# 88 sums moved from VectorE to GpSimd in a hybrid decoder layer

## The chip, the cores and the metric

One Trainium2 chip, of which the kernel uses one core. The metric is the device time of one execution in microseconds. TensorE (PE) multiplies matrices into PSUM; VectorE (DVE), ScalarE (ACT) and GpSimd (POOL) work on the on-chip memories; SyncE (SP) only starts transfers. GpSimd starts transfers too, in the order of its own instruction queue.

## The reference

One layer over 2048 tokens of width 1024, in float32. After an RMS norm, one projection `w_in` gives nine groups of columns; two branches are computed, each with its own gate, and merged:

```python
h = rms_norm(x, norm_g)
u = einsum('bsd,dc->bsc', h, w_in)
v_c, b_c, c_c, z_c, q, k, v, z_a, gate_logits = split(u)

y_c = b_c * causal_depthwise_conv(c_c * v_c, conv_w) * silu(z_c)     # 3 taps
y_a = y_c @ w_conv_out

q, k = rms_norm per head (16 query heads, 4 key heads, 64 wide)
o = sliding_window_attention(q, k, v, sinks) * silu(z_a)             # window 128, a sink per head
y_b = o @ w_attn_out

g_a, g_b = split(sigmoid(gate_logits + gate_b))
out = x + (g_a * y_a + g_b * y_b) @ w_out
```

## The kernel before

**Tiles and units.** The tokens are worked on in two tiles of 1024. Within a tile the work is a list of units, written out by hand in `SEQ0` and `SEQ1`: each unit multiplies the tile's activations by 256 columns of a weight. Tile two's list begins `ga0+ga1 k q0 v q1 q2 cv0 q3` (a pair with + is interleaved), so keys, values and the four query units stand at its beginning. The last units (`o`) multiply by `w_out`.

**Seven products instead of eight.** A unit's 1024 x 256 weights are four blocks, by two halves of the depth and two halves of the columns; the activations are four chunks in the same way. Instead of eight block products, the kernel does seven, by Strassen's scheme in Winograd's form: some products take a block, others a sum or difference of blocks. A product is 12 matmuls (4 chunks of depth, and 3 terms, since each float32 operand is cut into a rounded high part and a low remainder). `sunit` writes the products in the order 1, 5, 6, 2, 7, 3, 4 into the PSUM banks X, V and Y.

So each unit needs *weight sums*: four instructions on 128 x 512 elements, in place in the two raw tiles `ra` and `rb` of the unit's weights, made in `pieces_of`, `sums`. Each step needs the one before it. The first three make the two blocks of products 5 and 6 (pair `s`), the fourth ends those of 7 and 3 (pair `t`). Afterwards ScalarE rounds a pair (`w.._sh`, `w.._th`, L362) and VectorE takes the remainder (`w.._sl`, `w.._tl`). The V product (5) uses pair `s`.

The right-hand operands need *chunk sums* in the same way: `sums_of` makes them for a set of activations, four per pair of chunks, in two steps `first` and `second`, and stores each in the DRAM array `sd`, from which `load_set` reads them when the set becomes operands. The sets are `("c", t)`, the conv branch's output of tile t; `("a", t)`, the attention branch's; `("h", 1)`, the normed tokens of tile two (made in `h_prep` during tile one); and `("w", 0)`, `w_out` (made in `w_prep`). Their argument `eng` is the engine that issues the stores: SyncE for `"c"`, GpSimd for the others.

**What sets the order.** The program is a list of *ticks*, one a product. In `run`, each tick emits a product with its evacuation (`fin`), then the rounding of the next piece of weights on ScalarE, up to three functions planned for that tick, the piece's VectorE half (`lo`; a piece of kind `sums` has only this), further planned functions, loads on SyncE, and finally up to four *woven* steps: chains of small instructions, such as those of a reciprocal square root, which also advance by one with each VectorE instruction that goes through `vec`. Weight pieces run ahead of their products as far as eight ring buffers allow. Every engine takes its instructions in this order.

In the units of tile two that matter here, `fin_q` evacuates a quarter of a query unit, splits it (`q_h` on ScalarE, `q_l` on VectorE) and writes it to DRAM by four transfers on GpSimd's queue (`q2d`, L855); `fin_k` writes `rkd` (L921), reads it back as `k_r` (L932) and writes `kd` (L776); `fin_v` has TensorE transpose the values (`ptv`, L708) from `v_t` and writes `vd` (L957). Attention for tile two starts at unit q3; its flips and returns (`fd`, `x`, L1073 and L1080), its masks (`affine_select`, L1101) and its sums of halves (`od`, L1134) are GpSimd's too.

Lines of helpers: L480 is every matmul of a unit, L262 every VectorE instruction through `vec`, L297 the rounding of `split`.

Of the kernel before, what the change touches and what calls it, by code (L numbers as in the profile page):

```python
# [105 lines left out]
def block_kernel(  # L106
# [12 lines left out]
    nc = tc.nc  # L119
# [18 lines left out]
    def slot(shape, dt, name):  # L138
        return big.tile(shape, dt, tag="big", name=name)
# [160 lines left out]
    def add(o, a, b, eng=None):  # L300
        return (eng or vec).tensor_tensor(out=o, in0=a, in1=b, op=ALU.add)

    def sub(o, a, b, eng=None):
        return (eng or vec).tensor_tensor(out=o, in0=a, in1=b, op=ALU.subtract)
# [45 lines left out]
    def wpair(name):  # L350
        return [wpool.tile([P, KP * UC], F32R, tag="w", name=f"{name}{i}") for i in "hl"]

    def pieces_of(n):

        kind, srcs, key = plan[n]
        name = "w" + "_".join(str(i) for i in key)
        w = {}

        def two(hi, lo, src):
            return (lambda: nc.scalar.copy(hi, src),  # L362
                    lambda: vec.tensor_tensor(
                        out=lo, in0=src, in1=hi.bitcast(F32), op=ALU.subtract))

        if kind == "R":
            return w, []

        if kind:
            def pair(h, m1, m2, nm):  # L370
                hi, lo = (v.rearrange("p (i j c) -> p i j c", i=2, c=P) for v in wpair(f"{name}_{nm}"))
                for i, m in enumerate((m1, m2)):
                    w[m] = (hi[:, i], lo[:, i])
                return two(hi, lo, raws[2 * n + h])

            if kind == "P":
                return w, [(2, 1, lambda h=h: pair(h, (h, 0), (h, 1), f"p{h}")) for h in range(2)]

            def single():
                if n in paired:  # L380
                    hl = [slot([P, KP, P], F32R, f"{name}_d{i}") for i in "hl"]
                else:
                    d = wpool.tile([P, 2, KP, P], F32R, tag="w", name=f"{name}_d")
                    hl = [d[:, 0], d[:, 1]]
                w[4] = tuple(hl)
                return two(*hl, raws[2 * n + 1][:, 1])

            def sums():
                ra, rb = raws[2 * n], raws[2 * n + 1]

                def f():
                    sub(ra[:, 0], ra[:, 0], rb[:, 0])
                    summed.append(vec.chain(
                        lambda: add(rb[:, 0], rb[:, 0], rb[:, 1]),
                        lambda: sub(rb[:, 1], rb[:, 1], ra[:, 0]),
                        lambda: sub(ra[:, 1], ra[:, 1], rb[:, 1])))

                return (lambda: None, f)

            summed = []  # L400

            def of_sums(*args):
                summed[0]()
                return pair(*args)

            def single_sums():
                hi, lo = single()
                _, f = sums()

                def g():  # L410
                    lo()
                    f()

                return hi, g

            first = [(1, 0, single), (0, 0, sums)] if n not in paired else [(0, 0, single_sums)]
            return w, [(2, 0, lambda: pair(0, 1, 2, "a")), *first,
                       (2, 1, lambda: of_sums(1, 5, 6, "s")), (2, 1, lambda: of_sums(0, 7, 3, "t"))]
# [259 lines left out]
    def put(n, f):  # L678
        at.setdefault(max(n, tick[0] + 1), []).append(f)
# [525 lines left out]

    def sums_of(key, j, r, eng, n0=None):

        def first():
            sub(r[0, 0], r[0, 1], r[0, 0])
            eng.dma_start(sd[key][0, j], r[0, 0])  # L1210
            sub(r[0, 1], r[1, 1], r[0, 1])
            eng.dma_start(sd[key][2, j], r[0, 1])

        def second():
            sub(r[1, 1], r[1, 1], r[0, 0])
            eng.dma_start(sd[key][1, j], r[1, 1])
            sub(r[1, 0], r[1, 0], r[1, 1])
            eng.dma_start(sd[key][3, j], r[1, 0])

        if n0 is not None:  # L1220
            put(n0, first)
            put(n0 + 1, second)
        return second, first
# [43 lines left out]
    def fin_z(t, j, src, nm, key, to, at_of, eng):  # L1267
        got, left = {}, [4]
        second, first = sums_of(key, j, got, eng)
        steps = [lambda: put(tick[0] + 1 + SUM_WAIT, second), lambda: put(tick[0] + 1, first)]  # L1270

# [79 lines left out]
    def w_prep(n0):  # L1351

        for j in range(KP):
            r = {}

            def ld(j=j, r=r):
                for p in range(2):
                    for q in range(2):
                        r[p, q] = slot([P, H], F32, f"wo_{j}_{p}_{q}")
                        c = 2 * j + p  # L1360
                        nc.gpsimd.dma_start(r[p, q], w_o[c * P : (c + 1) * P, hs(q)])

            put(n0 + W_AT[j], ld)
            sums_of(("w", 0), j, r, nc.gpsimd, n0 + W_AT[j] + 4)
# [30 lines left out]
    def h_prep(t, n0):  # L1395
# [11 lines left out]
        for j in range(KP):  # L1407
            r = {}

            def ld(q, j=j, r=r):  # L1410
                if j < H_UP and q == 0:
                    for p in range(2):
                        two = upool.tile([P, 2 * H + 2], F32, tag="u", name=f"h{t}_{2 * j + p}")
                        for k in range(2):
                            r[p, k] = two[:, hs(k)]
                for p in range(2):
                    if j >= H_UP:
                        r[p, q] = slot([P, H], F32, f"h{t}_{q}_{2 * j + p}")
                    c = 2 * j + p
                    nc.gpsimd.dma_start(  # L1420
                        r[p, q], xt2[c * P : (c + 1) * P, t * T + q * H : t * T + (q + 1) * H])

            def norm(q, j=j, r=r):
                for p in range(2):
                    x_norm(r[p, q], 2 * j + p, rb[q])
                    if (p, q) != (0, 1):
                        nc.gpsimd.dma_start(hd[t][2 * j + p, :, hs(q)], r[p, q])

            n = n0 + 1 + H_AT[j]
            for q in range(2):  # L1430
                put(n + q, lambda q=q, f=ld: f(q))
                put(n + q + 3, lambda q=q, f=norm: f(q))
            sums_of(("h", t), j, r, nc.gpsimd, n + 7)
# [8 lines left out]
    for t in range(NT):  # L1442
# [9 lines left out]
        for word in (SEQ0, SEQ1)[t].split():  # L1452
            both_ = word.split("+")
            for name in both_:
                if len(both_) > 1:
                    paired.add(len(plan))
                key, j = name.rstrip("0123456789"), int(name[-1]) if name[-1].isdigit() else None
# [144 lines left out]
    kv = KV()  # L1602
# [161 lines left out]
```

## Time and profile before

| | |
|---|---|
| median of 3 runs | 1891.34 us (1890.53 to 1893.8) |
| the profiled execution's own time | 1890.92 us |
| its span, first to last instruction | 1889.2 us |
| TensorE, matmuls | 1880.8 us busy, granted clock 1.000 |
| TensorE, weight loads | 1565.5 us busy |
| VectorE | 1540.0 us busy, 2536 instructions |
| ScalarE | 989.0 us busy |
| GpSimd | 728.7 us busy, 1038 instructions |
| DMA | 435.81 MB, 231 GB/s on average |

Busy times are shares of one profiled execution, and engines overlap. GpSimd's busy time counts the issue of its transfers (0.5 to 1.1 us each), which is most of its 1038 instructions. The ends of TensorE's matmuls are modelled, so its busy share alone does not say how fast it goes. Tile one's units take the first half of the span; tile two's begin at about 878 us, its key, value and query units near 916 us, and `w_out` begins at 1733 us.

### The profile page before, as it was taken

The numbers are of one execution on the slowest core, as the hardware profiler recorded it, in microseconds if no ns is written. First come the engines' busy times: TensorE is split into PE (matmuls) and PEld (weight loads), VectorE is DVE, ScalarE is ACT, GpSimd is POOL, SyncE is SP. The second block draws the span as 40 slices with busy tenths as digits, with TensorE's granted clock in tenths as the row PEclk, the third lists the DMA queues.
The fourth block names the chain that finished last, engine by engine and source line by source line (L and its number), as shares of the span: only waits on it lengthen the run. The fifth ranks groups of instructions, "written<-read, shape, count | busy, mean of one in ns | idle before, by whom it ended". The sixth has DMA issues, their size and how long they took to land.

```text
span 1889.2 us, 27869 instructions
## 1 busy us (share of the span) xinstructions
PE 1880.8 (100%) x8638; PEld 1565.5 (83%) x8638; DVE 1540.0 (82%) x2536; ACT 989.0 (52%) x1993; POOL 728.7 (39%) x1038
## 2 busy tenths in 40 slices
PE   9999999999999999999999999999999999999999
PEld 7888888888888888888887888888888888888887
DVE  7989888789878889887579988888877789887654
ACT  7665554567665345435455645556566436344321
POOL 1472454456667111021075445656666311121000
PEclk9999999999999999999999999999999999999999
DMA  8475566689888978889367557768888869899653
GB/s 307 123 217 170 144 175 190 182 246 302 251 246 258 318 267 301 286 286 296 112 184 221 182 170 207 206 164 238 243 241 255 269 245 347 318 281 272 223 173 110
DMA packets 261189, 435.81 MB, mean 231 GB/s; under 512 B 33649, under 2 KB 124785, under 8 KB 261041
## 3 DMA queue, kind: packets, MB, share of 16 engines
q1 hardware_dynamic: 202848, 314.13, 50.3%
q0 software_dynamic: 58048, 119.87, 24.0%
q8 instruction: 69, 1.13, 0.3%
q14 instruction: 80, 0.65, 0.1%
q10 hardware_dynamic: 144, 0.03, 0.0%
HBM read 279.48 MB, written 154.42 MB: 230 GB/s over the span
## 4 chain that ended last, share of the span: by engine, by line
PE 82%; issue 7%; DVE 5%; DMA 3%; POOL 2%; ACT 1%; SPq 0%; POOLq 0%; DVEq 0%; ACTq 0%
PE Y L480 30%; PE Vcv L480 5%; PE Xcv L480 5%; PE po L1118 2%; PE Xgb L480 2%; PE Xb L480 2%; PE Vgb L480 2%; PE Xz L480 2%; PE Vb L480 2%; PE Vz L480 2%; PE Vo L480 2%; PE Xo L480 2%; PE Xza L480 2%; PE Vza L480 2%; PE Vga L480 2%
## 5 line engine op out<-in xcount | busy, mean ns | idle before, releaser
L1080 POOL DMA_DIRECT2D x<-fd x256 | 144.1, 614 | 69.7 <-DMA fd<-f 24.9
L1101 POOL TENSOR_SCALAR_AFFINE_SELECT xh<-xh 64x512 fp32r<-64x512 f32 x64 | 66.7, 1043 | 133.1 <-DVE xl L262 96.2
L1053 ACT ACTIVATE p<-s,st,rq 128x128 f32<-128x128 f32 x256 | 113.0, 451 | 5.7 <-DMA fd<-f 3.7
L1073 POOL DMA_DIRECT2D fd<-f x64 | 39.0, 610 | 176.6 <-DVE f L262 152.3
L480 PE MATMUL Xcv<-oph,wcv_ah 128*128 128x512 f32 x256 | 79.5, 392 | 0.0
L1134 POOL DMA_DIRECT2D od<-o x64 | 69.4, 1092 | 24.6 <-DMA od<-o 20.4
L855 POOL DMA_DIRECT2D q2d<-q_h x64 | 44.3, 692 | 84.3 <-ACT q_h L850 81.9
L1324 POOL DMA_DIRECT2D md<-thyb x32 | 27.4, 872 | 103.3 <-DVE thyb L262 87.7
L1101 POOL TENSOR_SCALAR_AFFINE_SELECT xl<-xl 64x512 fp32r<-64x512 f32 x64 | 64.3, 1004 | 4.4
L1101 POOL TENSOR_SCALAR_AFFINE_SELECT yp<-yp 64x512 fp32r<-64x512 f32 x64 | 55.7, 870 | 5.0 <-ACT yp L1088 0.9
L1101 POOL TENSOR_SCALAR_AFFINE_SELECT yp<-xl 64x512 fp32r<-64x512 f32 x64 | 56.1, 876 | 3.1
L480 PEld LDWEIGHTS Xcv<-oph,wcv_ah 128*128 128x128 f32 x256 | 47.3, 188 | 9.4
L262 DVE SCALAR_TENSOR_TENSOR y<-u,cols,y 128x512 f32<-128x512 f32 x64 | 51.5, 804 | 3.7 <-ACT y L1163 2.5
L262 DVE TENSOR_TENSOR p<-p,st 128x512 f32<-128x512 f32 x64 | 49.7, 776 | 2.6
L262 DVE TENSOR_TENSOR opa<-ina,opa 128x512 fp32r<-128x512 f32 x56 | 36.2, 686 | 18.3 <-ACT opa L297 18.3
L1053 ACT ACTIVATION_READ_ACCUMULATOR p<-s,st,rq 128x1 f32 x256 | 50.9, 199 | 0.0
L362 ACT CAST wcv_sh<-wcv_raw 128x1024 fp32r<-128x1024 f32 x16 | 16.8, 1053 | 63.5 <-DVE wcv_raw L262 63.5
L480 PE MATMUL Xcv<-oph,wcv_al 128*128 128x512 f32 x128 | 49.8, 389 | 0.0
L855 POOL DMA_DIRECT2D q2d<-q_l x64 | 44.1, 689 | 12.6 <-DVE q_l L262 9.9
L1028 PEld LDWEIGHTS s<-kq,q 128*128 128x128 f32 x256 | 45.9, 189 | 2.2
L262 DVE STREAM_TRANSPOSE f<-p 128x512 f32<-128x512 f32 x64 | 45.4, 710 | 2.7 <-DVE p L262 0.2
L262 DVE TENSOR_TENSOR opc<-inc,opc 128x512 fp32r<-128x512 f32 x56 | 36.1, 686 | 13.9 <-ACT opc L297 13.8
(774 smaller groups left out, 6611.5 us busy)
## 6 DMA issues: line engine op xcount, KB each, us to landing
wcv_raw<-in_w_in SPq DMA_DIRECT2D x32, 512.0 KB, 4.2
q<-q2d SPq DMA_DIRECT2D x64, 256.0 KB, 4.7
v<-vd SPq DMA_DIRECT2D x128, 128.0 KB, 4.7
fd<-f POOLq DMA_DIRECT2D x64, 256.0 KB, 3.8
x<-fd POOLq DMA_DIRECT2D x256, 64.0 KB, 3.6
gd<-th SPq DMA_DIRECT2D x64, 256.0 KB, 3.4
wq_raw<-in_w_in SPq DMA_DIRECT2D x16, 512.0 KB, 5.0
q2d<-q_h POOLq DMA_DIRECT2D x64, 128.0 KB, 3.7
```

Of the source, the lines that this page charges most:

```text
L262: r = f(*args, **kw)
L362: return (lambda: nc.scalar.copy(hi, src), lambda: vec.tensor_tensor(out=lo, in0=src, in1=hi.bitcast(F32), op=ALU.subtract))
L480: nc.tensor.matmul(ps, lhsT=w[:, j, :], rhs=b[:, m, :], start=start and j == 0 and i == 0, stop=j == KP - 1 and i == 2, skip_group_check=n ...
L855: nc.gpsimd.dma_start(q2d[t][j][half, q * 2 * HB : (q + 1) * 2 * HB, i, e, :], src[HALVES[e]].bitcast(F32).rearrange("p (b x) -> p b x", x ...
L1028: nc.tensor.matmul(sp[:, h, c, skip : 3 * HD], lhsT=q2[:, h, c, :], rhs=kq[:, 0, keys], start=False, stop=c == 1)
L1053: nc.scalar.activation(out=p[:, i, :], in_=sg[:, i, HD : 3 * HD], func=AF.Exp, bias=st[:, 1, i : i + 1], scale=rv[:, i // 2, i % 2 : i % 2 ...
L1073: nc.gpsimd.dma_start(fd, f)
L1080: nc.gpsimd.dma_start(x[QUADS[k]], src[k])
L1101: nc.gpsimd.affine_select(out=d4, in_=s4, pattern=[[0, 2], [-32 * sg, 2], [0, G], [-sg, 32]], compare_op=ALU.is_gt if prev else ALU.is_ge, ...
L1118: nc.tensor.matmul(po[:, cs], lhsT=v2[:, kind, :], rhs=xx[:, :, h * HD : (h + 1) * HD], start=h == 0 and n == 0, stop=n == 2, skip_group_c ...
L1134: put(tick[0] + ADD_WAIT, lambda: nc.gpsimd.dma_start(to, o[UH].rearrange("p c e q -> p (c e) q"), accum_op=ALU.add))
L1324: nc.gpsimd.dma_start(md[t][k, :, hs(q)], m, accum_op=ALU.add)
```

## The change

In `sums`, the four weight sums of tile two's key, value and query units (six units; `key[1]` is the tile) are given to GpSimd, all four in the tick of the piece, and nothing is left for the woven chain. The condition's `key[0] in "kv"` holds for `k` and `v` alone. In `sums_of`, the sums are given to GpSimd wherever GpSimd issues the stores: sets `("a", 0)`, `("a", 1)`, `("h", 1)` and `("w", 0)`, 16 sums each. `sub` and `add` with an engine given bypass `vec`, so no woven step advances with them. The arithmetic is the same.

```diff
@@ in pieces_of, sums
                 def f():
+                    if (key[0] == "q" or key[0] in "kv") and key[1] == 1:
+                        eng = nc.gpsimd
+                        sub(ra[:, 0], ra[:, 0], rb[:, 0], eng)
+                        add(rb[:, 0], rb[:, 0], rb[:, 1], eng)
+                        sub(rb[:, 1], rb[:, 1], ra[:, 0], eng)
+                        sub(ra[:, 1], ra[:, 1], rb[:, 1], eng)
+                        summed.append(lambda: None)
+                        return
                     sub(ra[:, 0], ra[:, 0], rb[:, 0])
                     summed.append(vec.chain(
                         lambda: add(rb[:, 0], rb[:, 0], rb[:, 1]),
@@ def sums_of(key, j, r, eng, n0=None)
+        on = nc.gpsimd if eng is nc.gpsimd else None
+
         def first():
-            sub(r[0, 0], r[0, 1], r[0, 0])
+            sub(r[0, 0], r[0, 1], r[0, 0], on)
             eng.dma_start(sd[key][0, j], r[0, 0])
-            sub(r[0, 1], r[1, 1], r[0, 1])
+            sub(r[0, 1], r[1, 1], r[0, 1], on)
             eng.dma_start(sd[key][2, j], r[0, 1])
 
         def second():
-            sub(r[1, 1], r[1, 1], r[0, 0])
+            sub(r[1, 1], r[1, 1], r[0, 0], on)
             eng.dma_start(sd[key][1, j], r[1, 1])
-            sub(r[1, 0], r[1, 0], r[1, 1])
+            sub(r[1, 0], r[1, 0], r[1, 1], on)
             eng.dma_start(sd[key][3, j], r[1, 0])
```

## The prediction

> **What bounds the kernel now.** I read the page's head first, then two rows of the table of stretches (the stretch, its length, busy time and instructions of TensorE, its weight load, VectorE, ScalarE and GpSimd, the granted clock, the DMA share and rate), then TensorE's waits (total, times, longest), then the chain of waits, of which one row stands here for the pace.
>
> ```profile
> span 1889.2 us, 27869 instructions
> PE 1880.8 (100%) x8638; PEld 1565.5 (83%) x8638; DVE 1540.0 (82%) x2536; ACT 989.0 (52%) x1993; POOL 728.7 (39%) x1038
> ```
>
> ```profile
> 600.00:650.00 50.00, 50.00 (x225) 41.39 (x224) 43.78 (x60) 19.55 (x31) 18.22 (x26) 1.00 0.92 303
> 950.00:1010.00 60.00, 58.62 (x264) 47.34 (x263) 48.91 (x90) 34.02 (x58) 47.00 (x77) 1.00 0.78 227
> ```
>
> ```profile
> PE Y L1498 <- DVE zero L181: 1.5, 1, 1.5
> PE Vq L480 <- DVE wq_sl L262: 0.7, 1, 0.7
> PE Y L480 <- DVE yap L262: 0.7, 1, 0.7
> PE Vv L480 <- DVE wv_sl L262: 0.4, 1, 0.4
> PE Vq L480 <- ACT wq_sh L362: 0.3, 1, 0.3
> ```
>
> ```profile
> 1749.51 5.44 PE Xo L480 x24
> ```
>
> TensorE runs wall to wall at a granted clock of 1.00. Busy time alone would not prove it, because the ends of matmuls are modelled; the pace does: 24 matmuls in a row in 5.44 us, 0.227 us each, and a product of twelve (one tick of the kernel's clock) 2.72 us. The five waits shown are together 3.6 us, 1.5 of them the kernel's start. So VectorE, 82% busy, is not the bound, and freeing it can return little more than the rest, 2.1 us or 0.11%. A loss has no such ceiling: whatever makes TensorE wait is added to the end. Three of the five are for exactly what the change moves: weights made from sums of tile two's values and queries (wv_sl, wq_sl, wq_sh). They lie in 950 to 1010, where TensorE lost 1.38 us and where GpSimd is busiest: 47 of 60 us. All figures are made against this execution, 1890.92 us, its span of 1889.2 and 1.72 around it; the median of the runs is 1891.34, 0.42 above.
>
> **Price of one moved sum.** On VectorE a 128x512 sum takes 0.69 us. GpSimd has done no two-input arithmetic in this kernel; its nearest rows are the selects of the attention.
>
> ```profile
> L262 DVE TENSOR_TENSOR wk_raw<-wk_raw,wk_raw x3: 678/692/693, 903.9 to 906.1; 128x512 f32<-128x512 f32 x3
> L262 DVE TENSOR_TENSOR wq_raw<-wq_raw,wq_raw x21: 668/691/694, 63.8 to 1033.6; 128x512 f32<-128x512 f32 x21
> L1101 POOL TENSOR_SCALAR_AFFINE_SELECT xh<-xh x64: 742/764/1692, 188.9 to 1475.4; 64x512 fp32r<-64x512 f32 x64
> L262 DVE TENSOR_TENSOR p<-p,st x64: 691/692/1240, 166.2 to 1453.7; 128x512 f32<-128x512 f32 x64
> ```
>
> The columns are shortest, median and longest duration in ns, and the first and last start. A select passes 512 elements of one operand in 0.76 us. Lower bound p = 0.75: the second operand is free. Upper bound 1.5: it costs a second pass; beyond that 1.7, the longest select, which was held up by something. I take p = 1.15, the middle of 0.75 and 1.5. [...]
>
> **Weight sums, 24 instructions (six units of four).** Removed from VectorE: 24 x 0.69 = 16.6 us, which TensorE does not feel. Added on GpSimd: 24 x 1.15 = 27.6 us, in order behind its DMA issues. Three sums must end before ScalarE rounds the first pair of sums (wq_sh, wv_sh) and VectorE takes the remainder (wq_sl, wv_sl), which the V product needs. So I look for the place of each unit's sums in GpSimd's queue. For keys (VectorE's sums at 903.9 to 906.1) and query 0, the next unit, the queue is empty: the first row below says GpSimd had been idle for 62.83 us at 947.61. For query 3 (VectorE sums to 1033.6) it is empty too, 21.76 us idle before 1044.58. There the sums start as soon as their operands are free, and cost nothing; without that cover it would be the lateness found next, 2.4 to 4.2 us a unit. For values, query 1 and query 2 the queue is full:
>
> ```profile
> 947.61 0.75 POOL L855 DMA_DIRECT2D q2d<-q_h  x1 [62.83 <-ACT q_h L850]
> ...
> 953.58 0.70 POOL L855 DMA_DIRECT2D q2d<-q_l  x1
> 954.27 3.88 POOL L921 DMA_DIRECT2D rkd<-k_rt  x8
> ...
> 964.65 0.53 POOL L932 DMA_DIRECT2D k_r<-rkd  x1 [0.48 <-DMA q2d<-q_l]
> 965.50 0.52 POOL L932 DMA_DIRECT2D k_r<-rkd  x1 [0.33 <-DMA q2d<-q_h]
> 966.40 2.69 POOL L932 DMA_DIRECT2D k_r<-rkd  x5 [0.39 <-DMA q2d<-q_l]
> 969.98 2.50 POOL L957 DMA_DIRECT2D vd<-v  x4 [0.89 <-DVE v L262]
> ...
> 996.75 0.69 POOL L855 DMA_DIRECT2D q2d<-q_l  x1 [0.24 <-issue]
> 997.43 0.61 POOL L776 DMA_DIRECT2D kd<-k_h  x1
> ...
> 1044.58 0.58 POOL L1073 DMA_DIRECT2D fd<-f  x1 [21.76 <-DVE f L262]
> ```
>
> ```profile
> 955.30 1.05 ACT L362 CAST wv_sh<-wv_raw 128x1024 fp32r<-128x1024 f32 x1 [2.55 <-DVE wv_raw L262]
> ...
> 973.24 1.05 ACT L362 CAST wq_sh<-wq_raw 128x1024 fp32r<-128x1024 f32 x1 [1.03 <-DVE wq_raw L262]
> ...
> 976.41 0.59 ACT L582 COPY v_t<-Y 128x512 f32<-128x512 f32 x1
> ...
> 996.68 1.05 ACT L362 CAST wq_sh<-wq_raw 128x1024 fp32r<-128x1024 f32 x1 [1.56 <-DVE wq_raw L262]
> ```
>
> ```profile
> 957.66 0.50 PE L480 MATMUL Vv<-oph,wv_sl 128*128 128x512 f32 x1 [0.41 <-DVE wv_sl L262]
> ...
> 977.83 0.60 PE L708 MATMUL ptv<-ident,v_t 128*128 128x128 f32 x4
> ...
> 999.23 0.50 PE L480 MATMUL Vq<-oph,wq_sl 128*128 128x512 f32 x1 [0.71 <-DVE wq_sl L262]
> ```
>
> ScalarE's rounding has no slack: each of the three already sat waiting for VectorE's sums, and everything behind it on ScalarE waits too.
>
> *Values.* In the program the sums follow the eight q2d issues of query 0's first two quarters, so they take the place of the rkd issues at 954.27. Three of them end at 954.28 + 3p = 957.73; ScalarE had them at 955.30. TensorE was already waiting for the result (0.41 at 957.66): late by 3p - 1.02 = **2.43 us**.
>
> *Query 1.* The four sums of values push the queue by 4p = 4.60. The waits in it (0.48, 0.33, 0.39, 0.89) take up 2.09 at most; v, for which vd waits, comes with TensorE 2.43 later. So the vd issues, which ended at 972.48, end between 975.0 (waits absorbed) and 976.2 (only the last); I take 975.5. Sums there at 975.5 + 3.45 = 978.95, against 973.24 + 2.43 = 975.67: 3.28 late. Behind that rounding on ScalarE stands v_t (ending 977.00), which TensorE's transposes at 977.83 need; about 0.6 of the 0.83 between is slack, the rest handing over. Left: **2.7 us**.
>
> *Query 2.* The sums come behind the eight q2d issues of query 1's first two quarters, the last of which ends at 997.44. By then everything has moved by the same 5.1, so the difference stays: 997.43 + 3p - 996.68 = 4.20. TensorE was waiting for wq_sh and wq_sl here: **4.2 us**. The kd and q2d issues behind are another 4.6 late, less the waits among them; the first attention block of tile two (its flip is at 1044.58) has slack for that.
>
> Sum 2.43 + 2.7 + 4.2 = 9.3; by p it is 9p - 1.0: 5.8 at 0.75, 12.5 at 1.5, 14.3 at 1.7.
>
> **Chunk sums, 64 instructions (32 attention branch, 16 next tokens, 16 w_out).** No DMA is added: the same sd stores stay on GpSimd's queue, and follow the sum on their own engine. GpSimd adds 64 x 1.15 = 73.6 us where it is idle: 18.2 of 50 us busy at 600 to 650. The store is about 0.5 us later per sum, and load_set reads it ten or more ticks (27 us) later. What is queued behind a sum waiting for VectorE's product is ocd, sd and md issues, all with ticks to spare; only the first next-token sums meet the tail of tile one's attention, whose selects come three ticks (8 us) before their product. Nothing, then; with that cover gone, two sums of 2.3 us ahead of a select. VectorE is relieved of 44 us that TensorE wasn't waiting for. I count 0, plus or minus 1. The forecast is 1890.9 + 9.3 = 1900.2, on the median's scale **1900.7 us**.
>
> **Rivals.**
> - *Waits vanish (not slower).* If GpSimd reaches a unit's sums when operands are free instead of after its DMA rows, the values' sums would be out near 950 to 952, ahead of 955.30, and the 1.38 us lost in 950 to 1010 comes back: 1889.5 (1889.9 on the median's scale). It decides at whether the first sum of values starts before 952. For it: three units find the queue empty. Against: the DMA rows before and after 954.27 stand back to back, and GpSimd's work is taken in order.
> - *Cheap and caught up.* p = 0.75, and the stalls at values and query 1 let the q2d queue drain before query 2, so that three issues fewer stand ahead of its sums, 3 x 0.69 = 2.1: 5.8 - 2.1 = 3.7, 1894.6 (1895.0 on the median's scale). For it: GpSimd is not busy for 13 of the 60 us from 950 to 1010. Against it: the waits named on its rows are for work that a stall delays too.
> - *Shared port.* The rows of the prices show VectorE's p<-p,st at 0.69 alone and up to 1.24, and selects from 0.76 to 1.69. If each sum and each two-input VectorE instruction hold each other up that much, p is 1.7 and VectorE gets back 88 x 0.55 = 48 of its 61 us: 14.3, and another 1 or so where VectorE's remainders are late: 1906. [...] Against it here: at all three places VectorE stands waiting for the rounding.
>
> **How the numbers follow.** Forecast 0.50 (1895.5 to 1904 by p from 0.75 to 1.5), waits vanish 0.16, cheap and caught up 0.20, shared port 0.14. This kernel's runs tell 0.2%, 3.8 us, from no change. Slower: all of the forecast, all of the port case, a fifth of the cheap one: 0.68. Faster: only the best third of the first rival, with gains elsewhere: 0.05. Same: 0.27. Range 1891.5 to 1907, which leaves out most of the first rival and the tail of the third.
>
> **What would show it.** Right: the sums of values start on GpSimd at about 954.3 and last 1.1 to 1.2 us; ScalarE's wv_sh and the two wq_sh wait longer than 2.55, 1.03 and 1.56; TensorE's waits on Vv, ptv and Vq grow to some 9 us between 950 and 1010, and nothing grows elsewhere. Wrong: no new TensorE wait there, sums that start under the DMA rows, a p outside 0.75 to 1.7, or waits in the stretches of the chunk sums.

## The result, and the profile after

The changed kernel takes 1938.59 us (median of four runs, 1935.51 to 1939.17); the kernel before takes 1892.57 us beside it (1890.53 to 1894.13). The ratio is 1.0241, with an interval of 1.0229 to 1.0253: 46.0 us slower, where 9.3 were forecast. The direction was right, and the time lies 32 us above the end of the range. The profiled execution took 1939.17 us, with a span of 1937.4, 48.2 longer than before.

The page's head, and then TensorE's waits (total, times, longest), of the changed kernel. Every line number above 400 has moved by 8 or 10.

```profile
span 1937.4 us, 27893 instructions
PE 1897.3 (98%) x8638; PEld 1571.5 (81%) x8638; DVE 1552.4 (80%) x2448; ACT 988.0 (51%) x1993; POOL 850.1 (44%) x1126
```

```profile
PE Vq L488 <- ACT wq_sh L362: 7.0, 1, 7.0
PE Vza L488 <- DVE wza_sl L262: 5.5, 6, 1.4
PE Vyb L488 <- DVE thya L262: 4.4, 1, 4.4
PE Vv L488 <- ACT wv_sh L362: 2.6, 1, 2.6
PE ptv L716 <- ACT v_t L590: 2.4, 1, 2.4
PE Vz L488 <- ACT wz_sh L362: 2.2, 1, 2.2
PE Vya L488 <- ACT zas L1294: 2.0, 1, 2.0
...
PE Vz L488 <- DVE wz_sl L262: 1.6, 2, 1.4
```

Three things are to be seen.

**The waits that were forecast are there, and others besides.** Vv, ptv and Vq wait 12.0 us for the weights of values, query 1 and query 2. Vza, Vyb, Vz and Vya wait 15.7 us (5.5 + 4.4 + 2.2 + 2.0 + 1.6), in units whose weight sums were not moved, for VectorE's remainders and evacuations or for ScalarE (wz_sh, zas), which had itself waited for VectorE there. All the waits of this view add up to 36.2 us; those of the kernel before add up to 4.6.

**VectorE did less and was busy longer.** It lost 88 instructions, 61 us at 0.69 each, but its busy time rose from 1540.0 to 1552.4. So what is left became 73 us longer, 0.83 us for each sum that moved. GpSimd's busy time rose by 121.4 us, 1.38 for each sum.

**Waits are not all of it.** 36.2 - 4.6 = 31.6 of the 48.2 us. For the rest, the table of stretches (the stretch, its length, busy time and instructions of TensorE, its weight load, VectorE, ScalarE and GpSimd, the granted clock, the DMA share and rate), where the clock granted to TensorE fell. In the kernel before it is 1.00 to the last matmul.

```profile
636.40:643.10 6.70, 6.09 (x14) 4.78 (x15) 6.70 (x5) 2.30 (x4) 5.79 (x6) 0.50 0.55 200
977.70:984.50 6.80, 6.34 (x14) 4.55 (x15) 5.14 (x6) 3.94 (x7) 6.80 (x13) 0.50 0.53 166
1005.00:1008.40 3.40, 3.40 (x10) 2.70 (x9) 2.59 (x9) 1.67 (x4) 2.11 (x4) 0.50 1.00 287
1028.90:1039.10 10.20, 6.10 (x14) 4.32 (x15) 5.57 (x7) 4.77 (x7) 9.96 (x13) 0.50 0.60 184
1711.60:1714.90 3.30, 3.28 (x8) 2.62 (x9) 2.28 (x4) 1.34 (x3) 0.00 (x0) 0.50 1.00 383
```

These five stretches, 30.4 us together, have a clock of 0.50. TensorE is busy in 25.2 us of them (6.09 + 6.34 + 3.40 + 6.10 + 3.28), and there a matmul starts 0.427 us after the one before it (nine in 3.84 us, from 979.97 to 983.81), where an unbroken row at full clock has 0.227. By these paces 0.47 of the busy time is lost, 11.8 us; taken as a half, here and below, some 12.6 us. With the 31.6 that is 44.2 of the 48.2.

**Where it was lost.** The 8638 matmuls come in the same order in both kernels, so the start of the same matmul in the two traces gives the delay gathered up to there. It is 0.8 us at 575 us of the kernel before, 18.6 at 850 to 900, 37.2 from 1025 to 1500 and 48.2 from 1675 on. So 18 us are lost in the second half of tile one, 18.6 at tile two's values to query 2, and 11.0 at its attention branch and `w_out`. The prediction put 9.3 on the second of these and nothing on the other two, where only chunk sums were moved. At the second the account closes: waits of 12.0, less the 1.4 that the kernel before had there, and half of the 15.8 us busy at half clock (6.34 + 3.40 + 6.10), together 18.5. At the other two it gives 21.0 + 4.7 = 25.7 of 29.6; some 4 us there stand in no wait of the list and in no stretch; "What stays open" comes back to them.

### The profile page after: what moved, and what is told of

The parts are those of the page before. It is cut to its first block, busy times and chain, and to the rows that moved or that the text cites. A ratio compares the mean times of both kernels' runs of the same rounds, so it can differ in the third digit from the quotient of the medians.

```text
span 1937.4 us, 27893 instructions
## 1 busy us (share of the span) xinstructions
PE 1897.3 (98%) x8638; PEld 1571.5 (81%) x8638; DVE 1552.4 (80%) x2448; ACT 988.0 (51%) x1993; POOL 850.1 (44%) x1126
## 4 chain that ended last, share of the span: by engine, by line
PE 76%; DVE 10%; DMA 6%; issue 4%; POOL 3%; ACT 1%; SPq 0%; DVEq 0%; POOLq 0%; ACTq 0%
PE Y L488 27%; PE Vcv L488 5%; PE Xcv L488 5%; PE Xb L488 2%; PE Vb L488 2%; PE Xga L488 2%; PE Xo L488 2%; PE Vo L488 2%; PE Vyb L488 2%; PE po L1126 2%; PE Vga L488 2%; PE Xyb L488 2%; PE Xgb L488 2%; PE Vgb L488 2%; PE Xz L488 2%
## 5 line engine op out<-in xcount | busy, mean ns | idle before, releaser
L1088 POOL DMA_DIRECT2D x<-fd x256 | 144.0, 606 | 72.9 <-DMA fd<-f 25.7
L262 DVE TENSOR_TENSOR opa<-ina,opa 128x512 fp32r<-128x512 f32 x56 | 41.4, 781 | 25.0 <-ACT opa L297 25.0
L262 DVE TENSOR_TENSOR opc<-inc,opc 128x512 fp32r<-128x512 f32 x56 | 51.7, 964 | 12.1 <-ACT opc L297 12.1
L304 POOL TENSOR_TENSOR zain<-zain,zain 128x512 f32<-128x512 f32 x32 | 46.6, 1457 | 27.0 <-DMA ocd<-zain 14.2
L863 POOL DMA_DIRECT2D q2d<-q_l x64 | 44.1, 690 | 12.6 <-DVE q_l L262 10.6
```

The source lines that it names most:

```text
L262: r = f(*args, **kw)
L863: nc.gpsimd.dma_start(q2d[t][j][half, q * 2 * HB : (q + 1) * 2 * HB, i, e, :], src[HALVES[e]].bitcast(F32).rearrange("p (b x) -> p b x", x ...
L1088: nc.gpsimd.dma_start(x[QUADS[k]], src[k])
```

## The experiments

Short diffs are against the changed kernel, unless the text says against the kernel before. "us more" is the difference of the medians from the kernel before in the same set of runs.

### The two halves of the change

Weight sums alone:

```diff
-        on = nc.gpsimd if eng is nc.gpsimd else None
+        on = None
```

> The 24 weight sums of tile two's keys, values and queries stay on GpSimd, the 64 chunk sums are back on VectorE. The two traces put 18.5 us of the loss between values and query 2 (lag of TensorE's matmuls against the kernel before grows from 18.8 to 37.3 us there) and 29.9 us at the chunk sums. Theory (two separate causes, each local): 1911, with the same three waits on wv_sh, v_t and wq_sh as after the change (2.6, 2.4, 7.0 us). Rival (one cause: GpSimd's chunk sums disturb VectorE and the lag at the weights is carried over from it): under 1896.

Measured: 1908.76 against 1892.36, ratio 1.0087 (1.0072 to 1.0102), 16.4 us more.

Chunk sums alone:

```diff
-                    if (key[0] == "q" or key[0] in "kv") and key[1] == 1:
+                    if False:
```

> The 64 chunk sums stay on GpSimd, the 24 weight sums are back on VectorE. Theory (local causes): 1892.6 + 29.9 = 1922, with waits of TensorE for wz_sh, wz_sl, wza_sl and thya as after the change, and none at values to query 2 beyond those of the kernel before. Rival (the chunk sums cost nothing by themselves, as the prediction had it): 1892 to 1894.

Measured: 1922.15 against 1892.36, ratio 1.0158 (1.0142 to 1.0173), 29.8 us more. The halves add up, 16.4 + 29.8 = 46.2 against 46.0, so they can be explained apart. TensorE's waits, of the weight sums alone and then of the chunk sums alone:

```profile
PE Vq L488 <- ACT wq_sh L362: 6.7, 1, 6.7
PE Vv L488 <- ACT wv_sh L362: 2.6, 1, 2.6
PE ptv L716 <- ACT v_t L590: 2.4, 1, 2.4
```

```profile
PE Vza L488 <- DVE wza_sl L262: 5.2, 5, 1.4
PE Vyb L488 <- DVE thya L262: 4.3, 1, 4.3
PE Y L488 <- DVE Vz L262: 3.4, 1, 3.4
```

The first three are the waits that the prediction named: 11.7 us, 10.3 more than in the kernel before. Behind each comes a stretch at half clock. The table of stretches of the weight sums alone:

```profile
958.90:965.50 6.60, 6.37 (x14) 4.59 (x15) 5.14 (x6) 3.74 (x7) 6.60 (x13) 0.50 0.56 168
986.20:989.40 3.20, 3.20 (x9) 2.42 (x9) 2.42 (x7) 1.44 (x4) 1.91 (x5) 0.50 0.95 294
1010.10:1016.70 6.60, 3.10 (x7) 1.99 (x8) 2.60 (x3) 3.82 (x6) 6.44 (x8) 0.50 0.43 114
```

TensorE is busy for 12.7 us at 0.50 (6.37 + 3.20 + 3.10), which loses 6.3; 10.3 + 6.3 = 16.6, against a span 16.3 longer. The second three are waits that the prediction had not.

### Which weight units cost

Keys, query 0 and query 3 alone, and query 2 alone, each with the chunk sums on VectorE:

```diff
+                    if key in (("k", 1), ("q", 1, 0), ("q", 1, 3)):
...
+        on = None
```

> Of all 88 sums only the 12 of tile two's keys, query 0 and query 3 are on GpSimd, the units where its queue was read as empty. Theory (place in the queue decides): nothing, 1892 to 1893. Rival (each weight sum costs by itself, by the port or by its 1.3 us): half of the loss of the weight sums alone, 1900.

Measured: 1892.09 against 1891.29, ratio 1.0003 (0.9993 to 1.0012). Twelve sums moved into an empty queue cost nothing that these runs can tell, and give nothing back.

```diff
+                    if key == ("q", 1, 2):
...
+        on = None
```

> Only the four sums of tile two's query 2 are on GpSimd. Theory (place in the queue, each unit by itself): behind the eight q2d issues that end at 997.43, three sums of 1.3 us end 4.65 us after VectorE's did (997.43 + 3.9 - 996.68), TensorE waits about that long for wq_sh, and its clock after it costs 2 to 4 us more: 1898 to 1901. Rival (the 7.0 us there were made by the backlog of values and query 1): a wait under 3 us, under 1896.

Measured: 1900.04 against 1891.29, ratio 1.0045 (1.0028 to 1.0062), 8.75 us more, over half of all six units. GpSimd's timeline of this kernel (start, duration), then ScalarE's:

```profile
999.04 0.59 POOL L784 DMA_DIRECT2D kd<-k_l  x1
999.70 1.26 POOL L304 TENSOR_TENSOR wq_raw<-wq_raw,wq_raw 128x512 f32<-128x512 f32 x1
```

```profile
1003.67 1.04 ACT L362 CAST wq_sh<-wq_raw 128x1024 fp32r<-128x1024 f32 x1 [8.83 <-POOL wq_raw L304]
```

The first sum starts at 999.70, behind the last of four `kd` issues of 0.6 us. My expectation, like the prediction, had it follow the last q2d issue, at 997.43. In the prediction's own row at 997.43 stands the first of those `kd` issues. ScalarE's rounding is 7.0 us later than before (1003.67 - 996.68), and TensorE's wait for the two parts of pair `s` rises from 1.0 (0.3 + 0.7) to 7.5.

### Is there time to be had by issuing the sums earlier

The four weight sums follow the remainder of the piece before, one tick earlier; the chunk sums are on VectorE:

```diff
+            def single_then():
+                hi, lo = single()
...
+                def g():
+                    lo()
+                    sub(ra[:, 0], ra[:, 0], rb[:, 0], nc.gpsimd)
...
+            first = [(1, 0, single_then if early else single), (0, 0, sums)] if n not in paired else [(0, 0, single_sums)]
```

> The 24 weight sums on GpSimd as in the run of the weight sums alone, but issued one tick earlier, right behind the remainder of the single block (w.._d), so that four to eight fewer transfer issues stand ahead of them in GpSimd's queue; the chunk sums are on VectorE. Theory (place in the queue): the wait for values goes (sums at 950.6 instead of 954.3 end before VectorE's did), those for query 1 and query 2 shrink to 2 us each or less: 1893 to 1898. Rival (GpSimd's 1.3 us instead of 0.69, wherever the sums stand): 1908 as before.

Measured: 1898.95 against 1891.32, ratio 1.004 (1.0026 to 1.0054), 7.6 us more instead of 16.4. The place in the queue is thus worth over half of the weight half, the clock included: one stretch of 3.4 us at 0.50 is left of three. TensorE's longest wait in this kernel:

```profile
PE Vq L498 <- ACT wq_sh L362: 3.2, 1, 3.2
```

It was 6.7; values and query 1 still wait 1.4 each. One tick is not enough to pass the block of issues.

### Why the chunk sums cost: do the two engines hold each other up

Both kernels here are the kernel before, with every sum on VectorE, and with work for GpSimd added beside each of the 64 chunk sums. In one it adds zeros in place, and so reads SBUF; in the other it only writes zeros. Neither delivers anything that anyone waits for.

```diff
+            for z in (lows[0][LH, 1], lows[0][UH, 0]):
+                nc.gpsimd.tensor_tensor(out=z, in0=z.bitcast(F32), in1=z.bitcast(F32), op=ALU.add)
```

> The kernel before, all 88 sums on VectorE; beside each of the 64 chunk sums GpSimd adds two 64x256 pieces of zeros to themselves in place (about 1.3 us in all), on which nothing depends. Theory (port: a GpSimd instruction that reads SBUF holds up VectorE's two-input instructions, and the other way round): as slow as the chunk sums alone or slower, since VectorE keeps its own sums too: 1915 to 1935. Rival (late data: GpSimd's sums end later than VectorE's did, and stores, buffers and loads behind them are late): nothing is late here, 1892 to 1894. Rival (occupancy: GpSimd's time itself, its transfers start later): a few us, and the same for the run that only writes.

```diff
+            kz = lows[0].bitcast(F32)
+            for _ in range(4):
+                nc.gpsimd.memset(kz[LH, 1], 0.0)
```

> As d_read, but beside each chunk sum GpSimd fills a 64x256 piece of zeros with zeros four times (about 1.3 us in all): the same occupancy, and nothing read from SBUF. Theory (port, by reads): 1892 to 1894. Rival (occupancy): as slow as d_read. Rival (port, by reads and writes alike): 1910 and more.

Measured: with reading, 1916.16 against 1892.36, ratio 1.013 (1.0113 to 1.0147), 23.8 us more. With writing, 1895.44, ratio 1.0015 (1.0006 to 1.0024), 3.1 us more. The groups (busy time, mean duration in ns) and tiles (shortest, median, longest duration in ns) of the reading kernel, then of the writing one:

```profile
L262 DVE TENSOR_TENSOR opc<-inc,opc 128x512 fp32r<-128x512 f32 x56 | 42.3, 797 | 7.9 <-ACT opc L297 7.9
L1209 POOL TENSOR_TENSOR lows<-lows x128: 601/950/1582, 605.9 to 1698.9; 64x256 fp32r<-64x256 f32 x128
```

```profile
L262 DVE TENSOR_TENSOR opc<-inc,opc 128x512 fp32r<-128x512 f32 x56 | 36.0, 687 | 13.2 <-ACT opc L297 13.2
L1210 POOL MEMSET lows<- x256: 304/307/852, 605.9 to 1677.9; 64x256 f32 x128
```

The same VectorE group, untouched by either edit, takes 797 ns on average where GpSimd reads and 687 where it writes; it was 686 in the kernel before. The two are not quite alike: the reading fills 121 us of GpSimd and the writing about 80. But 80/121 of 23.8 would be 16, not 3. And VectorE's busy time, for the same 2536 instructions, goes from 1540.0 to 1577.1 us with reading and to 1540.5 with writing. So GpSimd's reading of SBUF slows VectorE, and that costs TensorE time.

The 3 us of the writing kernel have another cause, and they show what GpSimd's queue alone can do. The matmuls' delay comes between 600 and 640 us. There the loads of the next tokens (`h`) stand behind the added work on GpSimd's queue. Three of them are issued at 613.08 in the kernel before (first row) and at 620.80 with writing (second row), and VectorE waits for them (third row):

```profile
613.08 1.59 POOL L1420 DMA_DIRECT2D h<-in_xt  x3 [2.03 <-issue]
```

```profile
620.80 1.61 POOL L1430 DMA_DIRECT2D h<-in_xt  x3 [4.61 <-issue]
627.50 0.75 DVE L262 SCALAR_TENSOR_TENSOR h<-h,cols,rb 128x512 f32<-128x512 f32 x1 [2.64 <-DMA h<-in_xt]
```

### One set of chunk sums, and the same spread out

The next tokens' 16 sums alone on GpSimd:

```diff
+                    if False:
...
+        on = nc.gpsimd if key[0] == "h" else None
```

> Only the 16 chunk sums of the next tokens are on GpSimd. The lag of the changed kernel grew by some 12 us where tile one's z units and these sums fall together (600 to 680), and by 6 more at the attention branch after. Theory (the port costs where VectorE is fullest, in the z units): 1900 to 1905. Rival (each of the 64 costs alike): 16 of 64, 1900 or less.

Measured: 1900.59 against 1891.29, ratio 1.0048 (1.0033 to 1.0063), 9.3 us more; a quarter of the 64 sums makes about a third of their loss. VectorE's timeline of this kernel, then GpSimd's:

```profile
634.87 3.98 DVE L262 TENSOR_TENSOR zin<-zin,zs 128x512 f32<-128x512 f32 x2
```

```profile
634.67 1.43 POOL L304 TENSOR_TENSOR h<-h 128x512 f32<-128x512 f32 x1
```

Two VectorE products, 1.28 us together in the kernel before, take 3.98 where GpSimd sums. The evacuation Vz stands behind them on VectorE, and TensorE waits 3.4 us for it in this kernel, as with all the chunk sums.

If bunching were the trouble, one sum per tick should help (the two edits above, and this):

```diff
+        if on:
+            for i in range(4):
+                put(n0 + i, lambda i=i: one(*STEPS[i]))
```

> The 16 chunk sums of the next tokens on GpSimd as in the run of these alone (1900.6), but each of the four of a pair of chunks in a tick of its own instead of two and two. Theory (the port: VectorE is held up several times in a row while the sums stand one behind the other; spread, each hold of 1.3 us finds slack): 1892 to 1896. Rival (what counts is the total that VectorE is held up): 1899 to 1902.

Measured: 1903.4 against 1891.32, ratio 1.0066 (1.0051 to 1.0081), 12 us more. It didn't help; if anything it cost more. The wait of 3.4 stays, and one of 2.6 comes beside it (those for wz_sl fall from 3.0 to 1.5). That fits a hold by each sum wherever it stands; bunching is not what costs.

### Does a wait cost more than its length

The kernel before, with dummy maxima on VectorE ahead of the evacuation of six `w_out` units, so that TensorE waits in a place that GpSimd has nothing to do with. First few, then many:

```diff
+    HOLD = {2: 2, 3: 4, 4: 5, 5: 6, 6: 7, 7: 9}
...
+        for _ in range(HOLD.get(key[1], 0) if key[0] == "o" else 0):
+            nc.vector.tensor_tensor(out=s5, in0=s5, in1=s5, op=ALU.max)
```

> The kernel before, with VectorE held up ahead of its addition of Y in six units of w_out (units 2 to 7) by 2, 4, 5, 6, 7 and 9 additional 128x512 maxima of s5 with itself (0.73 us each, the value stays): TensorE has to wait some 0, 1, 1.7, 2.4, 3.1 and 4.6 us there, 12.8 together. Theory (the half clock in the changed kernel is brought on by TensorE's own waits of over 2 us): the granted clock falls after the longer three or four waits, for 3 to 10 us each, and not after the shorter ones; 1905 plus 5 to 15. Rival (it came from the load or the transfers in that stretch): the clock stays at 1.00, 1905.

```diff
+    HOLD = {2: 9, 3: 9, 4: 10, 5: 10, 6: 11, 7: 13}
```

> As the run with VectorE held up ahead of the addition of Y, with 9, 9, 10, 10, 11 and 13 additional maxima in units 2 to 7 of w_out: by the waits measured there (2.6 us at nine, 0.73 a maximum) TensorE waits 2.6, 2.6, 3.3, 3.3, 4.0 and 5.5 us, 21 together. Theory (a wait that fills most of one period of about 3.4 us of a free-running check halves the clock for one or more periods; 2.6 us can fall across two and go free): the longer ones, above 3.3, always drop it, the 2.6 ones sometimes; 1891 + 21 + 5 to 10. Rival (waits alone don't drop it, a share of load in the stretch around values and query 2 did): the clock stays at 1.00 and the time is 1912.

Measured: the first, 1896.93 against 1891.29, ratio 1.0031 (1.002 to 1.0041), 5.6 us more. Its waits came out shorter than I had meant, three of 4.1 us together and 2.6 at most, and in the profiled execution the clock stayed at 1.00. That execution was the quickest of eight: five of the others have a mean granted clock of 0.999, where the kernel before has 1.000 in all 19, and they took 2.7 us longer on average than the three with 1.000. One period of 3.4 us at half clock would give a mean of 0.999. So this run hints at the theory and doesn't settle it. The second (two executions), 1926.94 against 1891.32, ratio 1.0187 (1.0167 to 1.0208), 35.6 us more. TensorE's waits for the evacuation in the second, and then a row of its table of stretches:

```profile
PE Y L480 <- DVE Vo L262: 21.3, 6, 5.5
```

```profile
1786.50:1789.80 3.30, 3.30 (x9) 2.62 (x8) 1.88 (x3) 0.00 (x0) 0.00 (x0) 0.50 0.29 107
```

Six waits of 2.6 to 5.5 us are 21.3 us, and the kernel lost 35.6. Every wait was followed by 3.4 or 6.8 us at half clock, with 25.0 us of busy TensorE in all, which loses 12.5: 21.3 + 12.5 = 33.8. So waits of this size cost more than their length, and waits alone bring the clock down: GpSimd has nothing to do in the row shown.

## Why the prediction was right and wrong

**Step "values": right.** The prediction had the sums start at about 954.3 and a lateness of 2.43 us. GpSimd's timeline of the changed kernel, then ScalarE's:

```profile
972.19 0.70 POOL L863 DMA_DIRECT2D q2d<-q_l  x1
972.90 1.31 POOL L304 TENSOR_TENSOR wv_raw<-wv_raw,wv_raw 128x512 f32<-128x512 f32 x1
```

```profile
976.94 1.04 ACT L362 CAST wv_sh<-wv_raw 128x1024 fp32r<-128x1024 f32 x1 [5.58 <-POOL wv_raw L304]
```

The sums stand behind the q2d issues, as read from the queue of before, and with the delay of 18.6 that the kernel has here already, 972.90 is 954.3. TensorE's wait went from 0.4 to 2.6, 2.2 more.

**Step "price": the term was too small.** p was set to 1.15; a sum takes 1.26 to 1.31 us when nothing disturbs it, and the next one starts 1.33 to 1.39 us after it. That is inside the bounds of 0.75 to 1.5. With p = 1.36, 9p - 1.0 gives 11.2 instead of 9.3. (The bounds on p give 1897.1 to 1903.8 on the median's scale; the 1895.5 that the prediction names as their lower end doesn't come out of its sum.)

**Step "query 1": near enough.** 2.7 forecast; TensorE waits 2.4 where it hadn't waited. The forecast's 0.2 us or so for handing v_t over was an estimate; here the transposes start 0.05 us after v_t ends (1004.47 to 1004.52). The hit is in part luck. The sums start at 996.64, which is 978.0 without the delay of 18.6 and 2.5 us later than the forecast 975.5. But TensorE had itself lost some 3 us by then, at half clock behind the wait for values (half of the 6.34), and the two nearly cancel.

**Step "query 2": the queue was read short.** Every issue that a moved step is put behind has to be counted. The prediction stopped at the q2d issues and wrote that the sums follow the last of them, though its own rows show a `kd` issue at 997.43, right behind them. Four `kd` issues stand there, 2.4 us. In the run of query 2 alone the rounding was 7.0 late: the 4.2 of the prediction, 2.3 for the later start (999.70 against 997.43), and 0.5 for the price of three sums. TensorE's wait rose by 6.5 there and by 6.0 here (from 1.0 to 7.0). The three places together are 10.6 us of new waits, against 9.3; the total came out nearer than its largest term, because the other two were a little less than forecast.

**Step "keys, query 0, query 3 cost nothing": right**, shown by that edit alone (1.0003).

**Step "chunk sums: I count 0, plus or minus 1": the step that failed, 29.8 us.** Its cover was GpSimd's idle time, 18.2 of 50 us busy. That cover is real and beside the point. The sums do not only use GpSimd: beside one, a VectorE instruction that takes both inputs from SBUF takes two to three times as long in the rows below, and VectorE is 82% busy with a TensorE behind it that has no slack. Around the wait of 4.4 us on Vyb, VectorE's timeline of the changed kernel, then GpSimd's:

```profile
1702.50 3.39 DVE L262 TENSOR_TENSOR opa<-ina,opa 128x512 fp32r<-128x512 f32 x2
1705.81 2.79 DVE L262 TENSOR_TENSOR wyb_sl<-wyb_raw,wyb_sh 128x1024 fp32r<-128x1024 f32 x1
1708.53 0.68 DVE L262 SCALAR_TENSOR_TENSOR thya<-thya,Y 128x512 f32<-128x512 f32 x1
```

```profile
1701.44 1.70 POOL L304 TENSOR_TENSOR wo<-wo,wo 128x512 f32<-128x512 f32 x1 [1.56 <-DMA wo<-in_w_out]
1704.03 1.30 POOL L304 TENSOR_TENSOR wo<-wo,wo 128x512 f32<-128x512 f32 x1
1706.21 1.30 POOL L304 TENSOR_TENSOR wo<-wo,wo 128x512 f32<-128x512 f32 x1
1708.39 1.33 POOL L304 TENSOR_TENSOR wo<-wo,wo 128x512 f32<-128x512 f32 x1
```

VectorE's timeline of the kernel before, at the same instructions:

```profile
1657.92 1.28 DVE L262 TENSOR_TENSOR opa<-ina,opa 128x512 fp32r<-128x512 f32 x2
1659.12 1.22 DVE L262 TENSOR_TENSOR wyb_sl<-wyb_raw,wyb_sh 128x1024 fp32r<-128x1024 f32 x1
```

From 1.28 and 1.22 to 3.39 and 2.79 is 3.7 us more, about three of the sums beside them. `thya<-thya,Y` keeps its 0.68 although the fourth sum runs beside it: its Y is in PSUM. Eight instructions of this kind (thya with a bank of PSUM) ran beside a sum in this kernel for 0.3 us or more, and none took more than 0.69; three transposes of key or query tiles, with a single input, ran beside one and took 0.68 to 0.72. Over the whole kernel the group opc, which no edit touched, goes from the first row (before) to the second (after). Of its 56 instructions, the 18 that overlap a sum take 1.56 us on average and 2.28 at most; the other 38 keep 0.68:

```profile
L262 DVE TENSOR_TENSOR opc<-inc,opc 128x512 fp32r<-128x512 f32 x56 | 36.1, 686 | 13.9 <-ACT opc L297 13.8
```

```profile
L262 DVE TENSOR_TENSOR opc<-inc,opc 128x512 fp32r<-128x512 f32 x56 | 51.7, 964 | 12.1 <-ACT opc L297 12.1
```

The reading and the writing kernel go the same way: with GpSimd reading SBUF opc takes 797 ns on average and the kernel loses 23.8 us, with GpSimd only writing it takes 687 and the kernel loses 3.1.

**The rival "shared port" had the cause, priced in the wrong place.** The runs show the holding up (opc 1.56 us beside a sum instead of 0.68, a sum up to 4.0 beside VectorE instead of 1.26 to 1.31); that a port does it is shown by none. The prediction held against it that VectorE stands waiting at the three places. That is so, and there the account closes without it. But the 64 chunk sums run in the stretches where VectorE is fullest. Its own figure, 0.55 us of VectorE for each sum, 48 for all 88, was of the right size (0.83 and 73 measured). The prediction offset it against the 61 us that VectorE gets back, as if a sum over the span counted. What counts is the place: time taken from VectorE right ahead of a remainder or an evacuation is taken from TensorE, and time given back elsewhere is not.

**Not in the sum: the granted clock.** Five stretches at half clock, some 12.6 us of the 48.2, and 6.3 of the 16.4 of the weight half.

**"What would show it"** named waits in the stretches of the chunk sums as the sign that the step was wrong. They are there.

**How one such delay travels.** Not every wait is next to a sum. Between 607 and 614 us sums of next tokens stretch VectorE's wz_sl to 2.79 us (1.23 before), and the zin products behind it are late. On SyncE the load of the next zin stands behind the stores of these products, so it leaves at 621.92 instead of 618.35; it also takes longer, and VectorE's product starts 9.1 us after it instead of 7.3. VectorE waits 4.11 us for it (0.26 in the kernel before), with the next weight sums behind it on its queue, ScalarE waits for those, and TensorE waits 2.2 and 1.4 us at 635. VectorE's timeline of the changed kernel, and ScalarE's:

```profile
610.99 2.79 DVE L262 TENSOR_TENSOR wz_sl<-wz_raw,wz_sh 128x1024 fp32r<-128x1024 f32 x1
...
631.03 0.69 DVE L262 TENSOR_TENSOR zin<-zin,zs 128x512 f32<-128x512 f32 x1 [4.11 <-DMA zin<-yd]
```

```profile
633.80 1.04 ACT L362 CAST wz_sh<-wz_raw 128x1024 fp32r<-128x1024 f32 x1 [5.89 <-DVE wz_raw L262]
```

**What stays open.** Some 4 of the 48.2 us, all at the chunk sums, are placed by no wait and no stretch. About 2.5 of them come from how a wait is counted: from the end of the matmul before it, 0.39 us after its start, while in an unbroken row the next would have started after 0.227. So each of the 18 waits that the changed kernel has more (26 against 8, of over 0.15 us each) costs up to 0.16 us beyond its length. Some 1.5 us remain without a row. And what share of the 29.8 us comes through late transfers, as in the last paragraph, and what share through VectorE directly, was not separated. The writing kernel, which holds up GpSimd's queue for some 80 us (the 64 chunk sums alone: 91) and leaves VectorE's instructions at their length, lost 3.1 us; so late issues on GpSimd's queue are likely a small part.

## What to carry to other kernels

An engine's idle time is no proof that it can take work for nothing. Ask whether the moved instruction holds up the engine that it relieves (here opc took 1.56 us beside a sum and 0.68 otherwise), and look whether the instructions that it lengthens stand right ahead of the one that sets the end. When a step moves to another queue, read that queue row by row up to the step's place: here four issues of 0.6 us, left out of the count, made a third of the longest wait. And a stall of a few microseconds on TensorE may cost half as much again in clock (35.6 us for 21.3 of waits).

## What the hardware showed that I had not expected

The granted clock fell to 0.50 after waits of 2.4 us, or of 2.2 and 1.4 close together, and stayed there for 3.4, 6.8 or 10.2 us. In the changed kernel the stretches begin at 636.34, 977.68, 1004.98, 1028.88 and 1711.54 us, which lie on one grid of 3.413 us (977.68 - 636.34 = 100 x 3.413). The grid tells what counts. In the 3.413 us ahead of each of the five starts TensorE was idle for 2.7, 2.3, 2.4, 3.0 and 3.4 us (for the second, from 975.41 to 977.68, the first part of its wait). The other traces can be put on their own grids, since each has at least one drop, if only one behind its last matmul. Over all thirteen, from 7 us after the start on, the least idle time in a period with a drop behind it is 1.83 us, in the writing kernel; the most in a period at full clock without one is 1.76, in the first clock experiment. Its wait of 2.6 us fell across two periods, 0.81 and 1.76. The rows of these two periods, the writing kernel's first; TensorE is busy for 1.58 and 1.65 of 3.41 us:

```profile
630.49:633.90 3.41, 1.58 (x6) 0.67 (x4) 3.38 (x5) 2.96 (x5) 0.64 (x2) 1.00 0.45 163
```

```profile
1878.74:1882.15 3.41, 1.65 (x7) 1.39 (x8) 2.16 (x4) 0.00 (x0) 0.00 (x0) 1.00 0.07 26
```

So the wait of 2.0 us on Vya brought no drop: the grid cuts it into 0.9 and 1.1. In the writing kernel two waits of 0.7 and 1.4 us, the second cut by the grid, brought one. In the changed kernel the half clock ended behind the first period with 0.08 us or less idle, and went on behind those with 0.49 or more. All these figures rest on the matmuls' modelled ends.

A GpSimd add or subtraction of 128x512 takes 1.26 to 1.31 us alone, and up to 4.0 beside VectorE: the longest starts at 1624.74 and spans six VectorE instructions, five of which keep their 0.68. The longest, in the view of tiles (shortest, median, longest in ns) of the changed kernel:

```profile
L304 POOL TENSOR_TENSOR zain<-zain,zain x32: 1282/1312/4023, 682.9 to 1649.2; 128x512 f32<-128x512 f32 x32
```
